# A 3x3 convolution on one core: four output pairs stored from ScalarE's DMA queue instead of one

## The chip, the core and the metric

The kernel runs on one core of one Trainium2 chip. The metric is device time in microseconds (us), as the median of several executions; the kernel before takes 127.07 us (three runs, 126.9 to 127.1). One execution was profiled, and all durations below come from it.

## The reference, cut to what matters

```python
x_pad = np.pad(x, ((0, 0), (0, 0), (1, 1), (1, 1)))       # x: 16 x 64 x 64 x 64, fp32
for b, co, ci, kh, kw:                                     # weight: 128 x 64 x 3 x 3, fp32
    output[b, co] += weight[co, ci, kh, kw] * x_pad[b, ci, kh:kh+64, kw:kw+64]
```

Sixteen images of 64 channels and 64x64 pixels are convolved with 128 filters of 3x3. 17.07 MB are read from HBM and 33.55 MB are written.

## The kernel before, in words

**Tiling.** Two images make a *pair*: their 2 x 64 channels fill the 128 partitions. There are eight pairs, and each is worked in two *halves*, so the main loop (line 206) has 16 steps (p, h). The vertical direction uses a small Winograd form, F(2,3): input rows are combined into sums (`ss`), differences (`dd`) and outer differences (`ee`) by GpSimd (lines 102 to 120; VectorE does it for the first half), and into an fp16 copy (`xh`, a cast on ScalarE, line 124). The filters are turned into seven fp16 matrices at the start.

**One half.** TensorE runs 54 matmuls into four PSUM tiles `pf1`, `pg1`, `pf2`, `pg2` of two banks each, all eight banks in total (lines 218 to 230). ScalarE makes three copies of PSUM tiles into `ut` (line 182), then the cast of the next half (line 226), then one copy straight into the output (line 234). VectorE makes the other three output rows by additions and subtractions (lines 231 to 233). All these instructions are kept in program order on their engine by `keep`. GpSimd works two halves ahead (line 208).

**Homes.** One SBUF tile `homes` has nine slots of 16 KB per partition. `X_HOME` says which slot holds pair p's input, and `O_HOME` which two adjoining slots hold its output. Slots are used again: the outputs of pairs 3, 4, 5 and 6 go to the slots that the outputs of pairs 0, 1, 2 and 3 left, those of pair 7 to a slot of pair 4's outputs and to the one where the input of pair 5 lay. So an output can be written only when the earlier store from its slot has landed.

**DMA order.** A DMA is issued by an engine's queue, in the order of that engine's program. SyncE (SP) issues the weights, the input of pair 0 in two parts, pairs 1 and 2, then pairs 3 and 4 as one transfer (line 72), all at the start. The inputs of pairs 5, 6 and 7 are issued from inside the loop, after the first halves of pairs 2, 3 and 4 (`NEXT_LOADS`, lines 53 and 237), since they take slots that other inputs must leave first. `store` (line 187) is called at the end of the second half of every pair. For the pairs in `BOTH` it is one transfer of 4 MB, for the others one transfer of 2 MB for each image. For pair 0 it is issued by ScalarE's queue, for all others by SP. In the second image of pair 5 the last seven rows are cut off and stored as 124 and 4 partitions (`FEW`). In the profile, SP's DMA queue is q1 and ScalarE's is q10.

Of the kernel before, what the change touches and what calls it, by code (L numbers as in the profile page):

```python
# [15 lines left out]
def kernel(  # L16
# [12 lines left out]
    nc = tc.nc  # L29
# [6 lines left out]
    keep = tc.keep_in_program_order  # L36
    x_rows = x.rearrange("b c h w -> (b c) h w")
# [10 lines left out]

    X_HOME = [0, 1, 2, 7, 8, 2, 7, 8]
    O_HOME = [5, 3, 0, 5, 3, 0, 5, 2]  # L50
    BOTH = (0, 3, 6)
    FEW = 5, 1, 7
    NEXT_LOADS = {(2, 0): 5, (3, 0): 6, (4, 0): 7}
    homes = slots.tile([128, 9, H, W], F32)
# [5 lines left out]
    def load(p, cuts=((0, H),)):  # L60
        for lo, hi in cuts:
            keep(
                nc.sync.dma_start(
                    xs[p][:, lo:hi, :], x_rows[128 * p : 128 * p + 128, lo:hi, :]
                )
            )
# [1 line left out]
    load(0, ((0, 34), (34, H)))  # L68
    load(1)
    load(2)  # L70
    rows = x_rows[128 * 3 : 128 * 5, :, :].rearrange("(g p) h w -> p g h w", g=2)
    keep(nc.sync.dma_start(homes[:, 7:9, :, :], rows))

    ident = const.tile([128, 128], F16)
    make_identity(nc, ident)
# [46 lines left out]
    def cast(p, h):  # L122
        t = cpool.tile([128, 17, W], F16, tag="xh", name="xh")
        keep(nc.scalar.copy(t, xs[p][:, C_ROW[h] : C_ROW[h] + 17, :]))  # L124
        return t

    def transforms(eng, p, h):
        return sums(eng, p, h), diffs(eng, p, h), outers(eng, p, h)
# [17 lines left out]
    def mms(tiles, terms, start, stop):  # L146
        n = 3 * len(terms)
        i = 0
        for wi, src, row in terms:
            for kw in (1, 0, 2):  # L150
                c_lo, c_hi = max(0, 1 - kw), min(W, W + 1 - kw)
                lo, hi = 0, RB
                at, step, rows = row
                while at + step * lo < 0:
                    lo += 1
                while at + step * (hi - 1) > rows - 1:
                    hi -= 1
                first, last = at + step * lo, at + step * (hi - 1)
                for b2 in range(2):
                    p0 = 64 * b2  # L160
                    keep(
                        nc.tensor.matmul(  # L162
                            tiles[:, b2, lo:hi, c_lo:c_hi],
                            Wt[p0 : p0 + 64, wi, kw, :],
                            src[
                                p0 : p0 + 64,
                                first : last + 1 : step,
                                c_lo + kw - 1 : c_hi + kw - 1,
                            ],
                            start=start and i == 0,  # L170
                            stop=stop and i == n - 1,
                            skip_group_check=not start,
                        )
                    )
                i += 1

    def acc():
        return psum.tile([128, 2, RB, W], F32, tag="acc", name="acc")

    def copied(tiles):  # L180
        ut = upool.tile([128, 2, RB, W], F32, tag="ut", name="ut")
        keep(nc.scalar.copy(ut, tiles))  # L182
        return ut
# [3 lines left out]
    def store(p, both):  # L187
        if p in BOTH:
            pair = out[2 * p : 2 * p + 2, :, :, :].rearrange("b c h w -> c b h w")

            eng = nc.scalar if p == 0 else nc.sync
            keep(eng.dma_start(pair, both))
            return
        for b2 in range(2):
            parts = [(0, CO, 0, H)]
            if (p, b2) == FEW[:2]:
                at = H - FEW[2]
                parts = [(0, CO, 0, at), (0, 124, at, H), (124, 4, at, H)]
            for c, n, lo, hi in parts:
                keep(  # L200
                    nc.sync.dma_start(
                        out[2 * p + b2, c : c + n, lo:hi, :], both[c : c + n, b2, lo:hi, :]
                    )
                )

    for n, (p, h) in enumerate(halves):
        if n + 2 < len(halves):
            tr[halves[n + 2]] = transforms(nc.gpsimd, *halves[n + 2])
        if h == 0:
            both = homes[:, O_HOME[p] : O_HOME[p] + 2, :, :]  # L210
            ov = both.rearrange("p b (j i) c -> p b j i c", i=2)
        ss, dd, ee = tr.pop((p, h))
        xc = xh.pop((p, h))
        jf, jg = RB * F_BLK[h], RB * G_BLK[h]
        sf, sg = jf - 16 * h, jg - 16 * h
        g_at = 2 * jg - C_ROW[h]

        pf1, pg1, pf2, pg2 = acc(), acc(), acc(), acc()
        mms(pf1, [(HP, ss, (sf, 1, 16))], True, True)
        ux = copied(pf1)  # L220
        mms(pg1, [(G1, ss, (sg, 1, 16))], True, True)
        ug = copied(pg1)
        mms(pf2, [(HM, dd, (0, 1, RB))], True, True)
        uy = copied(pf2)
        if n + 1 < len(halves):
            xh[halves[n + 1]] = cast(*halves[n + 1])
        mms(pg2, [(G01, xc, (g_at, 2, 17)), (G2, xc, (g_at + 2, 2, 17))], True, True)
        mms(pf1, [(G0, ee, (0, 2, 16))], False, True)
        mms(pg1, [(G21, xc, (g_at + 1, 2, 17)), (G0, xc, (g_at - 1, 2, 17))], False, True)
        mms(pf2, [(G2, ee, (1, 2, 16))], False, True)  # L230
        keep(nc.vector.tensor_add(ov[:, :, jg : jg + RB, 1, :], pg2, ug))  # L231
        keep(nc.vector.tensor_add(ov[:, :, jf : jf + RB, 0, :], pf1, uy))  # L232
        keep(nc.vector.tensor_sub(ov[:, :, jf : jf + RB, 1, :], ux, pf2))  # L233
        keep(nc.scalar.copy(ov[:, :, jg : jg + RB, 0, :], pg1))  # L234
        if h == 1:
            store(p, both)
        if (p, h) in NEXT_LOADS:
            load(NEXT_LOADS[p, h])

# [29 lines left out]
```

## Time and profile before

| what | value |
| --- | --- |
| median of three runs | 127.07 us |
| the profiled execution, its time | 126.95 us |
| its span, first to last instruction | 125.2 us |
| TensorE (PE) busy | 95.7 us |
| GpSimd (POOL) busy | 90.5 us |
| ScalarE (ACT) busy | 81.4 us |
| VectorE (DVE) busy | 63.9 us |
| DMA traffic | 50.77 MB, mean 406 GB/s |
| share of q1 (SP) and q10 (ACT) in the DMA engines' span | 88.6% and 7.9% |

The profiled execution's time is 1.75 us more than its span: what lies around the instructions. The page of the profile cuts the span into 40 slices of 3.13 us and gives a digit for the busy tenths of each engine, and under it the GB/s that the 16 DMA engines moved. The chain of waits follows the work back from the last instruction that an engine executed; transfers that are still running after that are not in it. The window view gives the same numbers for chosen stretches, the timeline lists instructions in order of time, and below it all the trace has a record of every packet that the DMA engines moved. In this kernel most packets are one row of 16 KB: one partition's 64x64 fp32 pixels.

### The profile page before, as it was taken

The page shows a single profiled execution, that of the slowest core. Times are in us where ns is not written, and L with a number is a line of the kernel's source. Part 1 is how long each engine was busy: PE and PEld are TensorE (multiplying, and loading weights), DVE is VectorE, ACT ScalarE, POOL GpSimd, SP SyncE. Part 2 cuts the span into 40 slices and gives each one's busy share as a digit, 9 for nine tenths or more (in the row PEclk, how much of TensorE's full clock was granted, in tenths as well). Part 3 has the DMA queues.
Part 4 walks back from the last instruction along what each step waited for, and adds up shares of the span by engine and source line. Part 5 has one row for each costly group of instructions (what it writes and reads, how often), then busy time and mean ns, then how long its engine had stood idle before and what let it go on. Part 6 is the DMA issues. An engine that isn't in the chain of part 4 may idle for free.

```text
span 125.2 us, 2157 instructions
## 1 busy us (share of the span) xinstructions
PE 95.7 (76%) x873; PEld 50.5 (40%) x873; DVE 63.9 (51%) x56; ACT 81.4 (65%) x86; POOL 90.5 (72%) x52
## 2 busy tenths in 40 slices
PE   0349999999999999999999999999999980000000
PEld 0224455455555555555555555555555530000000
DVE  0199657374939375674839393746647392000000
ACT  4457598599797978889897979788897940000000
POOL 2209999999999999999999999999999400000000
PEclk9999999999999999999999999999999997555555
DMA  4999999999999999999999999999999999999981
GB/s 125 375 454 424 429 429 429 435 335 419 424 429 435 435 419 429 403 437 440 437 411 382 440 424 419 429 440 424 435 419 431 426 414 436 429 440 435 419 372 58
DMA packets 3826, 50.77 MB, mean 406 GB/s; under 512 B 360, under 2 KB 488, under 8 KB 744
## 3 DMA queue, kind: packets, MB, share of 16 engines
q1 hardware_dynamic: 3544, 46.43, 88.6%
q10 hardware_dynamic: 272, 4.19, 7.9%
q8 instruction: 7, 0.11, 0.3%
q14 instruction: 3, 0.02, 0.0%
HBM read 17.07 MB, written 33.55 MB: 405 GB/s over the span
## 4 chain that ended last, share of the span: by engine, by line
PE 76%; DVE 3%; DMA 2%; POOL 1%; ACT 0%; issue 0%; DVEq 0%
PE acc L162 76%; DMA w_raw<-in_weight_dram 2%; DVE homes L233 1%; DVE ss L106 1%; POOL w L78 1%; DVE th L133 0%; DVE Wt L134 0%; PE wp L95 0%; ACT g0h L131 0%; DVEq L134 0%
## 5 line engine op out<-in xcount | busy, mean ns | idle before, releaser
L162 PEld LDWEIGHTS <-Wt 64*128 64x128 f16 x864 | 49.6, 96 | 47.0 <-issue 3.7
L182 ACT COPY ut<-acc 128x1024 f32<-128x1024 f32 x48 | 45.7, 1020 | 6.3 <-PE acc L162 6.3
L162 PE MATMUL acc<-xh,Wt 64*128 64x504 f16 (+3 forms) x384 | 46.3, 372 | 0.0
L106 POOL TENSOR_TENSOR ss<-homes 128x1024 f16<-128x1024 f32 x15 | 35.5, 2369 | 4.7 <-DMA homes<-in_x_dram 4.7
L231 DVE TENSOR_TENSOR homes<-acc,ut 128x1024 f32<-128x1024 f32 x16 | 19.6, 1225 | 32.2 <-PE acc L162 29.7
L119 POOL TENSOR_TENSOR ee<-homes 128x1024 f16<-128x1024 f32 x15 | 35.6, 2375 | 0.0
L162 PE MATMUL acc<-ss,Wt 64*128 64x504 f16 (+1 forms) x192 | 24.9, 392 | 2.3 <-DVE ss L106 2.3
L162 PE MATMUL acc<-ee,Wt 64*128 64x504 f16 (+1 forms) x192 | 26.5, 377 | 0.0
L234 ACT COPY homes<-acc 128x1024 f32<-128x1024 f32 x16 | 16.2, 1015 | 11.3 <-PE acc L162 10.7
L233 DVE TENSOR_TENSOR homes<-ut,acc 128x1024 f32<-128x1024 f32 x16 | 19.5, 1220 | 2.0 <-PE acc L162 1.4
L113 POOL TENSOR_TENSOR dd<-homes 128x512 f16<-128x512 f32 x15 | 20.2, 1347 | 0.0
L232 DVE TENSOR_TENSOR homes<-acc,ut 128x1024 f32<-128x1024 f32 x16 | 19.4, 1215 | 0.0
L124 ACT CAST xh<-homes 128x1088 f16<-128x1088 f32 x16 | 17.9, 1120 | 0.0
L162 PE MATMUL acc<-dd,Wt 64*128 64x504 f16 (+1 forms) x96 | 13.9, 392 | 0.0
L95 PE MATMUL wp<-ident,w 128*128 128x128 f16 x9 | 1.1, 309 | 4.6 <-POOL w L78 4.6
L133 DVE SCALAR_TENSOR_TENSOR th<-wp,g0h 128x384 f32<-128x384 f32 x1 | 0.6, 557 | 5.7 <-ACT g0h L131 5.7
L95 PEld LDWEIGHTS <-w 128*128 128x128 f16 x9 | 0.9, 158 | 4.6 <-POOL w L78 4.6
L119 DVE TENSOR_TENSOR ee<-homes 128x1024 f16<-128x1024 f32 x1 | 2.6, 2622 | 0.0
L78 POOL CAST w<-w_raw 128x576 f16<-128x576 f32 x1 | 0.7, 662 | 2.5 <-DMA w_raw<-in_weight_dram 2.5
L79 ACT CAST w<-w_raw 128x576 f16<-128x576 f32 x1 | 0.7, 672 | 1.8 <-DMA w_raw<-in_weight_dram 1.8
L79 ACT ACT_TABLE_LOAD x1 | 1.3, 1283 | 0.7 <-PEq L253 0.7
L106 DVE TENSOR_TENSOR ss<-homes 128x1024 f16<-128x1024 f32 x1 | 1.2, 1216 | 0.0
(15 smaller groups left out, 5.7 us busy)
## 6 DMA issues: line engine op xcount, KB each, us to landing
out_dram<-homes SPq DMA_DIRECT2D x9, 2048.0 KB, 17.5
homes<-in_x_dram SPq DMA_DIRECT2D x5, 2048.0 KB, 18.8
out_dram<-homes SPq DMA_DIRECT2D x2, 4096.0 KB, 22.2
homes<-in_x_dram SPq DMA_DIRECT2D x1, 4096.0 KB, 30.4
out_dram<-homes ACTq DMA_DIRECT2D x1, 4096.0 KB, 18.6
out_dram<-homes SPq DMA_DIRECT2D x1, 1824.0 KB, 23.6
homes<-in_x_dram SPq DMA_DIRECT2D x1, 1088.0 KB, 5.5
homes<-in_x_dram SPq DMA_DIRECT2D x1, 960.0 KB, 7.4
```

The costliest lines, as they stand in the source:

```text
L79: keep(nc.scalar.copy(w16[:, 1, :], w_raw))
L95: keep(nc.tensor.matmul(wps[kh][:, k * CO : k * CO + CO], w16[:, :, 3 * kh + k :: 9], ident))
L106: keep(eng.tensor_add(t, v[:, j : j + 16, 0, :], v[:, j : j + 16, 1, :]))
L113: keep(eng.tensor_sub(t, v[:, j : j + RB, 1, :], v[:, j : j + RB, 0, :]))
L119: keep(eng.tensor_sub(t, xs[p][:, r - 1 : r + 15, :], xs[p][:, r + 1 : r + 17, :]))
L124: keep(nc.scalar.copy(t, xs[p][:, C_ROW[h] : C_ROW[h] + 17, :]))
L162: nc.tensor.matmul(tiles[:, b2, lo:hi, c_lo:c_hi], Wt[p0 : p0 + 64, wi, kw, :], src[p0 : p0 + 64, first : last + 1 : step, c_lo + kw - 1 : ...
L182: keep(nc.scalar.copy(ut, tiles))
L231: keep(nc.vector.tensor_add(ov[:, :, jg : jg + RB, 1, :], pg2, ug))
L232: keep(nc.vector.tensor_add(ov[:, :, jf : jf + RB, 0, :], pf1, uy))
L233: keep(nc.vector.tensor_sub(ov[:, :, jf : jf + RB, 1, :], ux, pf2))
L234: keep(nc.scalar.copy(ov[:, :, jg : jg + RB, 0, :], pg1))
```

## The change

`BOTH` becomes (0, 2, 4, 6), and every store of these pairs is one 4 MB transfer issued by ScalarE's queue. It is no longer issued at the end of the pair but in the first half of the next pair, after the third PSUM copy and ahead of the cast. The pairs 1, 3, 5 and 7 stay on SP with one transfer for each image, pair 5 with its cut. The inputs of pairs 3 and 4 become two transfers. On SP, four stores and a merged load make way for that: between the input of pair 5 and that of pair 6 there is now no store, and between the stores of pairs 3 and 5 only the input of pair 7.

```diff
-    BOTH = (0, 3, 6)
+    BOTH = (0, 2, 4, 6)
...
-    rows = x_rows[128 * 3 : 128 * 5, :, :].rearrange("(g p) h w -> p g h w", g=2)
-    keep(nc.sync.dma_start(homes[:, 7:9, :, :], rows))
+    load(3)
+    load(4)
...
     def store(p, both):
         if p in BOTH:
             pair = out[2 * p : 2 * p + 2, :, :, :].rearrange("b c h w -> c b h w")
-
-            eng = nc.scalar if p == 0 else nc.sync
-            keep(eng.dma_start(pair, both))
+            keep(nc.scalar.dma_start(pair, both))
             return
...
         uy = copied(pf2)
+        if h == 0 and p - 1 in BOTH:
+
+            store(p - 1, before)
         if n + 1 < len(halves):
             xh[halves[n + 1]] = cast(*halves[n + 1])
...
-        if h == 1:
+        if h == 1 and p not in BOTH:
             store(p, both)
+        before = both
```

## The prediction

> **What bounds the kernel now.** I read the slices of the page first.
>
> ```profile
> PE   0349999999999999999999999999999980000000
> ...
> DMA  4999999999999999999999999999999999999981
> GB/s 125 375 454 424 429 429 429 435 335 419 424 429 435 435 419 429 403 437 440 437 411 382 440 424 419 429 440 424 435 419 431 426 414 436 429 440 435 419 372 58
> ```
>
> PE is full until slice 32 of 40 and then has nothing. The DMA engines are full from slice 1 to slice 37. The chain of waits is read next, with the one line that SP's timeline has after it:
>
> ```profile
> 8.09 94.56 PE acc L162 x864
> 102.64 0.02 issue
> 102.66 1.22 DVE homes L233
> ```
>
> ```profile
> 103.95 1.62 SPq L201 DMA_DIRECT2D out_dram<-homes  x2
> ```
>
> The chain says PE, but it ends at 103.9 us, and the span is 125.2. What comes after is the drain of stores. Is the drain late because the last store comes late, or because the queue is long? The windows tell:
>
> ```profile
> 38.00:48.00 10.00, 10.00 (x98) 5.38 (x96) 6.17 (x6) 8.20 (x10) 10.00 (x6) 1.00 1.01 431
> 104.00:120.00 16.00, 0.00 (x0) 0.00 (x0) 0.00 (x0) 0.00 (x0) 0.00 (x0) 0.52 1.01 433
> ```
>
> (The last column is GB/s.) The rate is 431 with compute running and 433 without, and at 433 the last pair's 4.19 MB need 9.7 us, yet they take about 19. So some 9 us of older stores stood ahead of them. In the trace's packet records no DMA engine has gaps of more than 0.6 us in total between 1.8 us and its end. **The bytes bound the kernel**: 50.77 MB at 430 GB/s are 118 us. Only three things can move the end: a hole in the DMA stream, slower packets, or a last DMA engine that ends at another time. The drain shows the third:
>
> ```profile
> 120.00:121.00 1.00, 0.00 (x0) 0.00 (x0) 0.00 (x0) 0.00 (x0) 0.00 (x0) 0.50 0.77 328
> 121.00:122.00 1.00, 0.00 (x0) 0.00 (x0) 0.00 (x0) 0.00 (x0) 0.00 (x0) 0.50 0.69 295
> 122.00:123.00 1.00, 0.00 (x0) 0.00 (x0) 0.00 (x0) 0.00 (x0) 0.00 (x0) 0.50 0.42 180
> 123.00:124.00 1.00, 0.00 (x0) 0.00 (x0) 0.00 (x0) 0.00 (x0) 0.00 (x0) 0.50 0.04 16
> ```
>
> The DMA shares sum to 1.92, so the engines end at 121.9 on average, while the last packet ends at 123.9: the span's end is that engine plus 1.3 us.
>
> **The change part by part.**
>
> *Bytes and transfers.* The bytes are the same, and so is the number of transfers, 24 (stores 15 to 14, input loads 8 to 9, weights 1). Cost 0.
>
> *Store 0, issued later.* Today:
>
> ```profile
> 21.37 1.01 ACT L234 COPY homes<-acc 128x1024 f32<-128x1024 f32 x1 [0.62 <-PE acc L162]
> 23.33 0.42 ACTq L192 DMA_DIRECT2D out_dram<-homes  x1
> 23.79 2.84 ACT L182 COPY ut<-acc 128x1024 f32<-128x1024 f32 x3 [1.41 <-PE acc L162]
> ```
>
> The issue waits for VectorE's last row, done at 23.24, and holds the three copies behind it from 22.66 (22.38 plus the usual 0.28) to 23.79. The change takes this 1.1 us from ScalarE; nobody gains, because PE has no gap there and is not the bound. After it the copies run 22.66 to 25.5 and the issue (0.42) starts between 24.5, when the third copy starts, and 25.5. Until the store's packets come, the engines have only the initial loads. Those would end at about 27.5: in the packet records an engine has six load packets of 0.61 us left at 23.9. Does the store come in time? The nearest start on idle engines is the weights: issued at 0.73, first packet 1.75, so 1.0 us; that gives 25.5 to 26.5, no hole. The store's own delay today is 3.75 us (23.33 to 27.08), which would give 28.3 to 29.3, a hole of 0.8 to 1.8 us. But this delay holds load packets that stood ahead on the same engines, and these are what ends at 27.5. I take the weights' row: **0, at most 1.8**. The Trainium skill ("DMA: Bandwidth & Descriptors", section "Latency and other measured facts") puts the first byte of a transfer issued by SP or ACT at about 0.6 us; by that the store would start by 26.1 and the sum would have no hole either, while the 3.75 of the trace speaks against reading 0.6 as the delay on loaded engines.
>
> *Change-over from loads to stores.* Where stores come in among loads, packets get slower:
>
> ```profile
> 25.30:27.00 1.70, 1.70 (x19) 0.86 (x17) 1.25 (x2) 1.70 (x3) 1.70 (x2) 1.00 1.10 337
> 27.00:28.50 1.50, 1.50 (x17) 0.86 (x15) 1.50 (x2) 1.50 (x3) 1.50 (x2) 1.00 0.92 350
> ```
>
> ```profile
> 65.00:69.00 4.00, 4.00 (x41) 2.12 (x39) 3.22 (x3) 3.10 (x4) 4.00 (x4) 1.00 0.98 389
> 78.00:83.50 5.50, 5.50 (x54) 2.89 (x52) 3.26 (x4) 4.60 (x6) 5.50 (x4) 1.00 1.01 432
> ```
>
> Against 430, the first two lose 1.7 x 93/430 + 1.5 x 80/430 = 0.65 us (store 0 on its own queue). Around 65 to 69 input 6 ends and store 3 begins in the same queue: 4 x 41/430 = 0.38. At 78 to 83.5 input 7 runs at full rate. After the change store 0 costs 0.65 again, or nothing if the loads are out. Store 2 now breaks in upon input 5 from the other queue: 0 (as input 7) to 0.65 (as store 0). Store 4 breaks in upon store 3, no load: 0. Inputs 6 and 7 alternate with stores; at 28.5 to 30, where both queues run, packets are back at 0.61 us, so 0 more. Bounds of the difference: -0.65 to +0.65. I take +0.3 for store 2, the middle, since neither row is nearer.
>
> *Input 7, later.* In the packet records both queues alternate packet by packet on one engine (store 27.2, load 27.8, store 28.5), so a store on q10 halves the pace of q1. Store 4 is issued with the third copy of (5,0), at 70.6 to 72, and begins by 71.6 to 75.7. At 74 q1 holds 9.4 us of store 3 and input 7 (its packets end at 83.4 now), and store 4 is 9.7 us: input 7's packets end near 93, at the latest 83.4 + 9.7 = 93.1.
>
> ```profile
> homes<-in_x_dram SPq DMA_DIRECT2D x1, 2048.0 KB, 21.9
> ```
>
> ```profile
> 86.46 2.36 POOL L106 TENSOR_TENSOR ss<-homes 128x1024 f16<-128x1024 f32 x1
> ```
>
> Issued at 63.07, it lands today at 85.0, and POOL takes it at 86.46: 1.5 us of slack. It will land at 91 to 94.7, so POOL stands still 4.5 to 8 us, and PE and ScalarE behind it (the cast of line 124 waits for it too, with the copies after it). POOL then needs 11.8 us for two halves, and 2.6 us of matmuls and 1.2 of VectorE follow: the last store is issued at 107 to 110 instead of 104. What hides it: stores 5 and 6 in the queues. Without it, an engine ends its last 9.7 us at the earliest at issue + 1.0 + 9.7, so 110 gives 120.7, before the 123.9 of the last engine. Cost 0; the cover is gone from 123.9 - 10.7 = 113 on.
>
> *Other waits.* Inputs 5 and 6 would land near 59 and 70, and POOL takes them at 62.97 and 74.72. Store 3 shares with store 4 and lands near 83; pair 6 writes its slots from 82.9: a second at most, inside the same cover. ScalarE's three new issues (0.42 each) fit in its 0.6 us of idle time per half.
>
> *The last engine.* It ends 2 us behind the mean by chance of slow packets (1.7 to 3.9 us of excess per engine) and by the cut of pair 5, which stays. Reshuffled: 0, at most 0.8 either way.
>
> **Sum**: 126.95 + 0 + 0.3 + 0 = 127.25; the median lies 0.12 above the profiled time, so 127.4.
>
> **The rivals.**
>
> *A, a hole behind the loads* (ScalarE's store reaches the engines 3.75 us after its issue even when they are idle): 127.07 + 0.3 + 1.3 = 128.7. For it: that delay. Against it: the load packets ahead.
>
> *B, smoother change-over, faster*: store 0 arrives just when the loads are out, at 27.5, and the 0.65 us of slow packets between 25.3 and 28.5 vanish; it decides if the first store packet comes right behind the last load packet. With store 2 at 0 and the last engine at half of its 0.8: 127.07 - 0.65 - 0.4 = 126.0. For it: the issue comes 1.2 to 2.2 us later, about as much as separates store 0's packets from the end of the loads. Against it: input 6's end, where the change-over inside one queue cost 0.38 as well.
>
> *C, input 7 uncovers the end*: if the last store is issued after 113, each us costs one. PE's granted clock falls from 1.00 to 0.50 at 104.8, 2 us after its last matmul, and in its first 4.5 us (8.0 to 12.5) PE got through 22 matmuls where later 72 took 7.4 us, half the pace. A stall of 5 us could so add 2 us of PE, 112 in all, and a bit more makes 127.07 + 0.3 + 1.5 = 128.9. The Trainium skill (same page, "Queues, rings and completion order") says that a DMA engine goes round its queues packet by packet; the alternation in the records agrees, and it is this rule that delays input 7.
>
> *D, the chain of waits is right and PE's end counts*: +4 us, 131. Against it: 9 us of queue ahead of the last store.
>
> **Chances.** Forecast 0.52 (own range 126.7 to 128.0), A 0.14, B 0.22, C 0.08, D 0.04. This kernel's measurement can tell 0.2%, 0.25 us. Of the forecast's part 0.10 are faster, 0.14 within, 0.28 slower; so faster 0.10 + 0.22 = 0.32, within 0.14, slower 0.28 + 0.14 + 0.08 + 0.04 = 0.54. The range reaches from B at 126.0 past A and C to 129.2, which is A with its full 1.8.
>
> **What would show it.** DMA slices at 9 throughout with q10 at four times its share; no dip to 0 near 28 us; POOL waiting 4 to 8 us for an input near 86; SP's last store at 107 to 110; the drain at 430 GB/s, ending near 124. A dip near 28 means A, full rate from 25 to 28 means B, empty slices near 111 mean C. I am wrong in kind if the rate itself changes where both queues run.

## The result, and the profile after

The changed kernel takes 128.8 us (median of four runs, 128.17 to 129.14) where the kernel before took 126.98 on the same chip (four runs, 126.73 to 127.10): a ratio of 1.0149, 95% interval 1.012 to 1.0178. Timed again on another chip it took 128.14 (127.12 to 131.21, eight runs) against 126.83: 1.0059 (1.0025 to 1.0092). The two intervals do not meet; the change costs 0.6 to 1.5%, and its executions lie further apart than those of the kernel before. All ratios here leave out executions more than 1.5% above the fastest of their kernel; three experiments (store 4 alone, store 6 back on SP, useless matmuls) had such an execution profiled, and it is used for what its trace shows, not for its time.

The profiled execution took 128.17 us, with a span of 126.4. The page's slices of it:

```profile
PE   0339999999999999999999999999921999940000
...
POOL 2209999999999999999999999995008998000000
PEclk9999999999999999999999999999996579999555
DMA  4999999999999999999999999999999989989992
GB/s 110 382 436 441 430 436 420 425 389 441 446 425 415 415 420 420 371 410 430 438 412 436 425 425 436 420 430 430 415 441 421 428 310 443 420 332 410 415 415 104
```

PE has a hole at slices 29 and 30 (92 to 98 us), POOL one just ahead of it, and PE's granted clock is down behind it. PE has nothing in the last four slices; before, it had nothing in the last seven. The DMA row has what it did not have before: two digits below 9 in the middle, slices 32 and 35, where the rate is 310 and 332 GB/s; slice 35 begins at 110.6 us, and empty slices near 111 were the prediction's sign for rival C. Slice 8 (25 to 28 us), where store 0 comes in, is at 389 instead of 335; slice 16 (51 to 54), where store 2 now breaks in upon input 5, is at 371. The queues' shares went where the change sends them: q10 from 7.9 to 31.4%.

The DMA issues of 63 to 64 us and the timeline behind them (start, duration, engine, instruction; in brackets the idle time before it and what ended it):

```profile
homes<-in_x_dram SPq DMA_DIRECT2D x1, 2048.0 KB, 31.5
```

```profile
95.19 2.35 POOL L106 TENSOR_TENSOR ss<-homes 128x1024 f16<-128x1024 f32 x1 [8.13 <-DMA homes<-in_x_dram]
97.58 2.74 PE L162 MATMUL acc<-ss,Wt 64*128 64x512 f16 x12 [5.06 <-POOL ss L106]
101.70 0.38 ACTq L190 DMA_DIRECT2D out_dram<-homes  x1
113.42 2.35 SPq L199 DMA_DIRECT2D out_dram<-homes  x2
```

Input 7, issued at 63.55, lands after 31.5 us, at 95.05 (before: 85.0). POOL stands still for 8.13 us, PE for 5.06 behind it. ScalarE stands too, and so it issues store 6 at 101.70, though the last row of pair 6 was done at 93.79 (VectorE, 92.57 + 1.22). The last store is issued at 113.42; I call this time T, and in the kernel before it was 103.95.

The windows (busy time and count of PE, PEld, DVE, ACT and POOL, then PE's clock, DMA share, GB/s):

```profile
50.00:54.00 4.00, 3.98 (x38) 1.67 (x36) 3.01 (x3) 3.09 (x4) 4.00 (x2) 1.00 0.99 358
95.00:101.00 6.00, 3.42 (x18) 1.36 (x19) 0.00 (x0) 3.66 (x4) 5.82 (x3) 0.58 1.01 429
101.00:104.00 3.00, 3.00 (x22) 1.34 (x20) 0.24 (x1) 2.38 (x3) 3.00 (x3) 0.69 0.82 297
...
111.00:113.00 2.00, 1.09 (x12) 0.29 (x6) 1.83 (x2) 1.01 (x1) 0.00 (x0) 1.00 0.89 369
113.00:115.00 2.00, 0.00 (x0) 0.00 (x0) 0.35 (x1) 0.00 (x0) 0.00 (x0) 1.00 0.74 303
```

At 101 to 104 the DMA engines run partly dry (share 0.82) because store 6 is not yet issued, at 111 to 115 because store 7 is not. PE did 18 matmuls in 3.42 us at a clock of 0.58; from 104 to 111, at 1.00, it did 67 in 6.92.

To set the losses against each other I take the *lag*: the time, less the bytes moved by then at 430 GB/s (from the packet records of q1 and q10). The records do not name the engine; the engines' ends and gaps are put together from them, packet behind packet, and the idle times are good to some 0.2 us.

| | before | after |
| --- | --- | --- |
| lag at 24, 30, 50, 54 us | 2.86, 3.58, 3.73, 3.84 | 2.97, 3.16, 3.41, 4.13 |
| lag at 70, 100 us | 4.31, 4.47 | 4.30, 4.54 |
| lag at 104, 112, 118 us | 4.57, 4.56, 4.54 | 5.41, 5.50, 6.53 |
| idle time of one DMA engine, 100 to 118 us | about 0 | about 1.4 |
| the engines' ends, mean and last (the prediction's mean, 121.9, came from shares) | 122.27, 123.86 | 124.30, 125.11 |

By 100 us nothing is lost on balance: what store 0 gained, store 2 took. Then 0.9 us go ahead of store 6 and 1.0 ahead of store 7, and the mean engine ends 2.0 us later. The last engine ends only 1.25 later, since the wait for the last store evens the engines out.

### The profile page after: what moved, and what is told of

Same layout as the page of the kernel before. It is cut to its first block, busy times and chain, and to the rows that moved or that the text cites. A ratio compares the mean times of both kernels' runs of the same rounds, so it can differ in the third digit from the quotient of the medians.

```text
span 126.4 us, 2158 instructions
## 1 busy us (share of the span) xinstructions
PE 99.6 (79%) x873; PEld 45.8 (36%) x873; DVE 64.1 (51%) x56; ACT 81.7 (65%) x86; POOL 90.6 (72%) x52
## 3 DMA queue, kind: packets, MB, share of 16 engines
q10 hardware_dynamic: 1088, 16.78, 31.4%
## 5 line engine op out<-in xcount | busy, mean ns | idle before, releaser
L162 PEld LDWEIGHTS <-Wt 64*128 64x128 f16 x864 | 44.8, 97 | 61.0 <-issue 12.5
L162 PE MATMUL acc<-xh,Wt 64*128 64x504 f16 (+3 forms) x384 | 47.2, 380 | 0.0
L162 PE MATMUL acc<-ss,Wt 64*128 64x504 f16 (+1 forms) x192 | 26.0, 407 | 7.5 <-POOL ss L106 5.1
L235 ACT COPY homes<-acc 128x1024 f32<-128x1024 f32 x16 | 16.2, 1012 | 14.0 <-PE acc L162 12.1
L162 PE MATMUL acc<-dd,Wt 64*128 64x504 f16 (+1 forms) x96 | 14.5, 409 | 0.1
## 6 DMA issues: line engine op xcount, KB each, us to landing
homes<-in_x_dram SPq DMA_DIRECT2D x7, 2048.0 KB, 24.6
```

Of the source, the lines that this page charges most:

```text
L162: nc.tensor.matmul(tiles[:, b2, lo:hi, c_lo:c_hi], Wt[p0 : p0 + 64, wi, kw, :], src[p0 : p0 + 64, first : last + 1 : step, c_lo + kw - 1 : ...
```

## The experiments

Two theories stood first. **C**, from the prediction: store 4 makes something in SP's queue late, and through that the last store (the expectations call it L). **M**, its rival: a second queue with large stores costs time as such. Two experiments undo the lateness in different ways, a third brings it about with store 4 alone.

*Input 7 on ScalarE's queue, ahead of store 4* (from the changed kernel):

```diff
-    NEXT_LOADS = {(2, 0): 5, (3, 0): 6, (4, 0): 7}
+    NEXT_LOADS = {(2, 0): 5, (3, 0): 6}
...
             store(p - 1, before)
+        if (p, h) == (4, 1):
+            keep(nc.scalar.dma_start(xs[7], x_rows[128 * 7 : 128 * 8, :, :]))
```

> The changed kernel, with input 7 issued by ScalarE's queue in the second half of pair 4, ahead of store 4 in the same queue, and no longer by SP. All four stores stay on ScalarE's queue. Theory L (input 7 is late because store 4 halves the pace of its queue, so PE stalls and the last store is issued at 113.4 instead of 104): input 7 lands near 82, POOL waits for no input after the first, the last store is issued near 104, no hole in the DMA stream after 100, time 126.5 to 127.3. Rival M (two queues that mix loads and stores cost packets their pace, or stores on ScalarE's queue cost as such): the mixing is still there, 128.3 to 129.0.

Measured: 126.72 us (126.49 to 127.49, ten runs) against 126.74, ratio 0.9998 (0.9977 to 1.002). Its list of waits, and its timeline:

```profile
DVE homes L234 <- DMA out_dram<-homes: 9.0, 2, 6.3
```

```profile
86.50 2.41 POOL L106 TENSOR_TENSOR ss<-homes 128x1024 f16<-128x1024 f32 x1
111.82 2.60 SPq L199 DMA_DIRECT2D out_dram<-homes  x2
```

POOL takes input 7 at 86.50 without a wait, and all of the loss is gone, although four stores still go by ScalarE's queue. T is not back at 104, however: VectorE waits 6.3 us for store 3 to leave the slots that pair 6 writes, since store 3 now shares the engines with store 4. So store 4 delays two things. At T = 111.82 a delay costs nothing.

*Store 4 back on SP* (from the changed kernel):

```diff
-    BOTH = (0, 2, 4, 6)
+    BOTH = (0, 2, 6)
```

> The changed kernel with pair 4 out of BOTH, so that store 4 goes by SP behind input 7, as two transfers at the end of the pair. Theory L: input 7 lands near 85 as before the change, the last store is issued near 104, time 126.6 to 127.4. Rival M: one of four stores less on ScalarE's queue, so about a quarter of the 1.8 us is gone: near 128.3.

Measured: 126.79 (126.56 to 127.31, ten runs) against 126.74, ratio 1.0003 (0.9984 to 1.0023). Its timeline:

```profile
86.39 2.38 POOL L106 TENSOR_TENSOR ss<-homes 128x1024 f16<-128x1024 f32 x1
104.04 1.58 SPq L199 DMA_DIRECT2D out_dram<-homes  x2
```

POOL takes input 7 at 86.39 without a wait, VectorE has no wait for a store either, and T is that of the kernel before. Stores 0, 2 and 6 on the second queue, with their later issue, cost nothing. M falls: with input 7 ahead of store 4, or with store 4 back on SP, nothing is paid, so the price hangs on store 4 running beside the input 7 that waits on SP. The Trainium skill ("DMA: Bandwidth & Descriptors", section "Issuing engines are not separate DMA queues") says that transfers started by several engines share the same DMA engines, and that this saves only time of issuing; both runs agree in that the second queue gained nothing (0.9998 and 1.0003).

*Store 4 alone on ScalarE's queue* (from the kernel before):

```diff
         uy = copied(pf2)
+        if (p, h) == (5, 0):
+            pair = out[8:10, :, :, :].rearrange("b c h w -> c b h w")
+            keep(nc.scalar.dma_start(pair, before))
...
-        if h == 1:
+        if h == 1 and p != 4:
             store(p, both)
+        before = both
```

> The kernel before, with the one difference that store 4 is issued by ScalarE's queue behind the third copy of (5,0), as one transfer. Theory L: input 7 lands near 95 and the last store is issued near 113, as in the changed kernel, so this one move brings all of the loss: 128.2 to 129.0. Store 6 is issued by SP at the end of its pair, so a hole near 102 is not expected. Rival M: one quarter of the loss, near 127.4.

Measured: 131.58 (128.57 to 133.02, four runs) against 126.74; the runs lie too far apart for an interval. The DMA row of its page (span 131.2) and its timeline:

```profile
DMA  5999999999999999899999999999999799615995
```

```profile
90.87 1.23 DVE L234 TENSOR_TENSOR homes<-acc,ut 128x1024 f32<-128x1024 f32 x1 [8.60 <-DMA out_dram<-homes]
100.98 2.34 POOL L106 TENSOR_TENSOR ss<-homes 128x1024 f16<-128x1024 f32 x1 [12.59 <-DMA homes<-in_x_dram]
119.05 0.83 SPq L201 DMA_DIRECT2D out_dram<-homes  x2
```

One moved store is enough: even the shortest of the four executions, 128.57, is 1.4% above the kernel before. In the profiled one, the longest, input 7, issued at 64.97, lands 6 us later than in the changed kernel: by the semaphore records the 16 engines finished their parts of it between 91.4 and 100.8, and the landing is that of the slowest. T is 119.05, and the DMA row falls to 1 ahead of the last store.

*Input 7 late by order alone* (from the kernel before; nothing but store 0 on ScalarE's queue):

```diff
-    NEXT_LOADS = {(2, 0): 5, (3, 0): 6, (4, 0): 7}
+    NEXT_LOADS = {(2, 0): 5, (3, 0): 6, (4, 1): 7}
```

> The kernel before with one difference: the load of input 7 is issued behind store 4 in SP's queue (after (4,1) instead of after (4,0)). No store moves to ScalarE's queue and no queues mix. Theory L: input 7 lands near 85.0 + 9.7 = 94.7 as in the changed kernel, GpSimd waits 8 us for it, the last store is issued at 111 to 113.5 and the time rises by 0.3 to 1.6 us over the kernel before, to 127.1 to 128.4. Rival M (mixing queues is the cost): no change, 126.6 to 127.0.

Measured: 127.03 (126.87 to 127.72, ten runs) against 126.66, ratio 1.0027 (1.0002 to 1.0051). Its timeline, and its windows:

```profile
95.12 2.34 POOL L106 TENSOR_TENSOR ss<-homes 128x1024 f16<-128x1024 f32 x1 [8.38 <-DMA homes<-in_x_dram]
113.30 0.83 SPq L201 DMA_DIRECT2D out_dram<-homes  x2
```

```profile
111.00:113.00 2.00, 0.98 (x10) 0.27 (x6) 1.83 (x2) 1.01 (x1) 0.00 (x0) 1.00 0.52 221
```

In a single queue, by being put behind store 4, input 7 is as late as in the changed kernel (95.12 and 95.19), T is the same (113.30 and 113.42), and the DMA engines run dry for about 1.9 us each ahead of store 7. The time lies between the two expectations and decides nothing by itself; the trace does. This is C without a second queue. It costs 0.27%, less than the change, so the lateness of input 7 is not the whole price. In the profiles the difference lies in the last engine: all 16 engines end within 0.16 us (124.00 to 124.16), where in the changed kernel the mean is 124.30 and the last 125.11.

*The two remedies together* (input 7 on ScalarE's queue, and `BOTH = (0, 2, 6)`):

> The changed kernel with both remedies: input 7 is issued by ScalarE's queue in the second half of pair 4, and store 4 goes by SP at the end of its pair. So neither input 7 nor store 3 shares its time with store 4. Theory L: neither GpSimd nor VectorE waits for a transfer after the first, the last store is issued at 104 to 106. The run with input 7 on ScalarE's queue had moved 0.5 us more of bytes than the kernel before at 100 us, and lost it in the stalls behind store 3; without them the time is 126.2 to 126.5 where the kernel before has 126.7. If the last of the 16 engines decides whatever the mean does: 126.5 to 127.0, no difference.

Measured: 127.14 (126.38 to 128.03, twelve runs) against 126.86, ratio 1.0021 (0.9987 to 1.0054). The expected gain did not come. T was 106.92, as VectorE still waited 4.0 us for store 3, beside which input 7 now ran. The lag at 100 us was 4.32, against 4.47 before; the last engine ended at 124.19, 2.1 us behind the mean. In this execution, what the stream gained, the last engine took back.

Two dry places were seen in the changed kernel, ahead of store 6 and ahead of store 7. Three experiments are meant to close them.

*Store 6 back on SP* (from the changed kernel):

```diff
-    BOTH = (0, 2, 4, 6)
+    BOTH = (0, 2, 4)
```

> The changed kernel with pair 6 out of BOTH: store 6 goes by SP at the end of its pair instead of behind the third copy of (7,0). The changed kernel has two holes in the DMA stream, 0.8 us at 101 to 104 (store 6 not yet issued) and 1.1 us at 112 to 116 (store 7 not yet issued). Theory L with the end set by the last store's issue alone: the first hole closes, the second grows by as much, the last store is still issued near 113, time 128.3 to 129.0. Rival H (each hole counts by itself): 0.8 us less, near 128.0.

Measured: 127.87 (126.86 to 130.16, ten runs) against 126.74, ratio 1.0066 (1.0037 to 1.0094). The hole at 101 to 104 is closed (lag 5.09 at 100, 5.22 at 104), but in its profiled execution VectorE waited 5.1 us for store 3 and POOL 10.8 for input 7, T was 116.26, and the engines then lay dry ahead of store 7 instead, about 3.8 us each.

*Pair 7 stored in two halves of 32 rows* (from the changed kernel), so that half of the last bytes is issued one half earlier:

```diff
-        if h == 1 and p not in BOTH:
+        if p == NP - 1:
+            lo = 32 * h
+            for b2 in range(2):
+                keep(nc.sync.dma_start(out[2 * p + b2, :, lo : lo + 32, :], both[:, b2, lo : lo + 32, :]))
+        elif h == 1 and p not in BOTH:
             store(p, both)
```

> The changed kernel, with the rows 0 to 31 of pair 7 stored at the end of its first half, and only the rows 32 to 63 at the end of its second. Input 7 is as late as in the changed kernel. Theory L (the end is the last store's issue plus what it moves, about 9.7 us of packets): what the last issue carries is halved to 4.9 us, and the earlier half fills the hole at 112 to 116; the hole at 101 to 104 (0.8 us) stays, so the time falls by about 1 us, to 127.4 to 128.0. Rival M (two queues that mix loads and stores cost the pace): no change, 128.4 to 129.0.

Measured: 127.99 (127.45 to 129.8, four runs) against 126.83, ratio 1.0088 (1.0053 to 1.0123). That is at the upper end of what was expected, and too near to the 128.14 of the changed kernel on the same chip to show a gain.

*Both together*:

> The changed kernel with both edits together: pair 6 is stored by SP in two transfers at the end of the pair (as in the run of store 6 on SP), and pair 7 in two halves of 32 rows, the first after (7,0) (as in the run of the early store 7). Input 7 and store 3 still come late. Theory U, the late input uncovers the DMA engines in two places, ahead of store 6 (its issue stands behind ScalarE's stalled copies, 0.8 us lost at 101 to 104 in the changed kernel's profile) and ahead of store 7 (1.0 us at 112 to 116), and closing one leaves the other to grow: with both closed the median is 126.7 to 127.3, ratio 0.999 to 1.004, and the moved bytes lag by no more than 0.4 us more at 118 than at 100, though POOL still waits 8 to 11 us for input 7. Rival R, something else about a second queue with four stores costs the time (slower packets, a more ragged end): the median stays at 127.8 to 128.3 as with either edit alone, ratio 1.006 or more.

Measured: 127.83 (127.52 to 128.71, six runs) against 126.59, ratio 1.0102 (1.006 to 1.0144). Its DMA row, and its list of waits:

```profile
DMA  4999999999999999999999999999999999999970
```

```profile
POOL ss L106 <- DMA homes<-in_x_dram: 14.7, 2, 9.7
```

The holes are gone, as the DMA row shows (idle time of an engine from 100 to 118 us: about 0), though POOL waits 9.7 us, and yet the time is not back. Theory U falls by its own measure, and the time is the one that rival R named; but R's reason, four stores on the second queue, does not fit input 7 on ScalarE's queue, where all four stores go that way at no price. In this execution the mean engine ended at 122.48, 0.2 later than before, and the last at 124.41, 0.55 later. Part of that may come from the experiment itself, whose last packets are rows of 8 KB instead of 16. So the dry engines are not the whole price, and what the rest is stays open.

*Useless matmuls ahead of (7,0)'s first ones* (from the changed kernel), to hold PE's clock up; they write a PSUM tile that the right matmuls then start afresh:

```diff
+        if (p, h) == (7, 0):
+            for _ in range(7):
+                mms(pf1, [(G1, xc_old, (0, 1, 17))], True, True)
         mms(pf1, [(HP, ss, (sf, 1, 16))], True, True)
```

> The changed kernel, with 42 matmuls of no use ahead of the first ones of (7,0), into the tile that these then overwrite: PE has work while GpSimd waits for input 7. Theory L with the clock in it (the stall of 5 us lets PE's clock fall to half, and (7,0) takes 8.3 us instead of 5.8): (7,0) takes about 6 us, the last store is issued near 111.5 instead of 113.4, and the time falls by 1 to 2 us, to 127.0 to 127.8. Rival (the clock has no part, GpSimd's two halves set the pace after input 7): 128.4 to 129.0.

Measured: 128.56 (126.81 to 131.02, ten runs) against 126.83, ratio 1.0084 (1.0048 to 1.0119). This is not the 127.0 to 127.8 that was expected, but it is inconclusive: in its profiled execution pair 6 waited for store 3, and the useless matmuls ran at 97.71 to 102.43, not inside the stall.

*The changed kernel again*:

> The changed kernel once more, so that the other kernels of this call have it beside them on the same chip: 128.2 to 129.1, with the last store issued near 113. Since input 7 has landed only when the slowest of the 16 DMA engines is through with it, single executions may be longer.

Measured: 128.14, as told above, just under what was expected. Its profiled execution (127.61 us, span 125.8) tells more about the clock than the experiment before it. Its timeline:

```profile
88.56 0.82 PE L162 MATMUL acc<-ss,Wt 64*128 64x512 f16 x6 [3.29 <-DVE homes L232]
95.89 2.36 POOL L106 TENSOR_TENSOR ss<-homes 128x1024 f16<-128x1024 f32 x1 [9.08 <-DMA homes<-in_x_dram]
98.30 1.47 PE L162 MATMUL acc<-ss,Wt 64*128 64x512 f16 x12 [1.73 <-POOL ss L106]
111.86 2.72 SPq L199 DMA_DIRECT2D out_dram<-homes  x2
```

POOL starts 0.7 us later than in the first profile, but PE had been delayed by store 3 and stood only 1.73 us before (7,0); the twelve matmuls take 1.47 us, not 2.74, and T comes 1.56 us earlier. Here the clock was lost as well, from 89.6 to 93.0, behind the 3.29 us for store 3, but it was back before (7,0). From POOL's start to T the first profile needs 18.2 us and this one 16.0: the clock lost in (7,0) was worth some 2.3 us of T.

Two experiments look at the change-over from loads to stores near 25 us.

*Store 0 behind the cast of (1,0)* (from the kernel before):

> The kernel before, with store 0 alone moved: it is issued by ScalarE's queue behind the cast in (1,0), at about 26, instead of 23.3, and as one transfer as before. By the cumulated bytes the changed kernel lost 0.4 us less than the kernel before at 25 to 30, where store 0 comes in among the last loads. If that is the change-over and nothing else gives it back: 126.2 to 126.5 where the kernel before has 126.74 on the same chip, 0.3 us less. If the last of the 16 DMA engines sets the end whatever the mean does: no difference, within 0.2%.

Measured: 126.71 (126.41 to 127.36, twelve runs) against 126.83, ratio 0.9992 (0.9974 to 1.001). It tells little, since the issue came at 23.63 and not near 26: ScalarE issued the DMA before the third copy (24.09) and the cast (24.99), which stand ahead of it in its program, had started.

*Store 0 on SP's queue too* (from the kernel before, so that all transfers share one queue):

> The kernel before with store 0 on SP's queue too, behind the initial loads: nothing is stored by ScalarE's queue and no two queues run side by side. Over the runs so far, the loss around 25 to 30 fell from about 0.9 us where store 0 was issued at 23.2 to 23.6 to 0.2 us where it was issued at 24.6 to 24.95. In one queue the change-over is that of input 6 and store 3, 0 to 0.4 us. Theory: the mean of the DMA engines gains 0.3 to 0.6 us and the time falls to 126.1 to 126.5, where the kernel before has 126.8. If the last of the 16 engines decides whatever the mean does: 126.5 to 126.9, no difference. Rival M (ScalarE's queue costs as such): the gain would be about a quarter of the change's loss, 0.3 us, and would show in the rate beyond 30 us.

Measured: 127.11 (126.45 to 128.35, twelve runs) against 126.66, ratio 1.0033 (1.0 to 1.0067); the gain that was expected did not come. Its window where store 0 comes in:

```profile
26.00:28.00 2.00, 2.00 (x22) 1.07 (x20) 2.00 (x2) 1.38 (x2) 2.00 (x1) 1.00 1.08 311
```

The slow packets are there in one queue as well: the lag grows by 0.81 us from 24 to 30, against 0.72 in the kernel before. The change-over is not a matter of the second queue.

## Why the prediction was right, and where it was wrong

The time, 128.8, lies inside the range of 126.0 to 129.2, and its side, slower, had the largest chance. But the likeliest case did not come. The time is that of **rival C** (128.9), which had 0.08, and the signs are C's. That the side and the range held is luck in good part: 0.28 of the 0.54 for slower were the forecast's own, which went by a loss at the change-over that came out at 0, and the range reached as far as 129.2 for rival A's sake.

*What bounds the kernel: right.* At 70 and at 100 us the lag of the two kernels is the same within 0.1, although the order of the transfers differs.

*Store 0, cost 0: right.* No hole came behind the loads. It was issued at 24.93, inside the 24.5 to 25.5 that were given, and the windows from 24 to 28.5 have 415 GB/s. Rival A fell.

*Change-over, +0.3: its size was wrong.* Store 0 lost 0.2 instead of 0.7 us, store 2 upon input 5 lost 0.7 (4 x 72/430, the row of 50 to 54). In the second profile of the same kernel it was the other way round (1.0 and 0.03). The sum, by the lag at 70 us, is 0 (4.30 and 4.24 against 4.31). Each of the two stores came out towards an end of its bounds of 0 to 0.65, or beyond it, and at opposite ends in the two profiles. Of rival B's gain of 0.65 the first profile had 0.5, and store 2 ate it; the second had none.

*Input 7, "cost 0": this is the step that failed.* Its mechanism was right: alternation packet by packet (from 76 to 92 us q1 and q10 moved some 200 and 225 GB/s), a stall of POOL, a late last store. Three of its terms were too small:

- The landing. "91 to 94.7" was worked out with the mean backlog of an engine, but a landing is the slowest engine's. The 16 engines finished their parts between 82.3 and 85.0 in the kernel before and between 89.9 and 95.0 here, so the spread grew from 2.7 to 5.1 us. It landed at 95.05, and at 95.2 to 100.8 in six other executions of kernels with store 4 on ScalarE's queue and input 7 behind it.
- The clock. It stood in rival C only. PE's clock was at half from 96.0 to 102.8; the first 36 matmuls of (7,0) took 6.47 us (97.58 to 104.05), those of (6,1) 3.81 (86.61 to 90.42), so 2.66 were lost. 95.19 + 11.8 + 2.6 + 1.2, the prediction's own sum, gives 110.8; the clock makes it the 113.42 that was measured, 3.4 us beyond the upper end of "107 to 110". The Trainium skill ("TensorE: Matmul & The Clock Gate", Part 1) has the clock fall to half after an idle window of about 3.4 us; the traces agree roughly: stalls of 5.06, 3.29 and (input 7 on ScalarE's queue) 3.13 us lost the clock, those of 1.86 (store 6 back on SP) and 1.73 did not.
- The cover. "Stores 5 and 6 in the queues" was to hide it, but store 6 was not in its queue. Its issue stands behind ScalarE's copies, ScalarE stood with PE, and it came at 101.70, 7.9 us after pair 6's last row. I had written that the stall reaches ScalarE, and had not followed it to the DMA that ScalarE issues behind its copies.

*"The cover is gone from 113 on": nearly right.* Here T is the last store's issue in the profiled executions of the kernels that change the late part of the stream and keep pair 7's store whole:

| kernel | T | span | span less T |
| --- | --- | --- | --- |
| before | 103.95 | 125.2 | 21.3 |
| store 4 back on SP | 104.04 | 125.0 | 21.0 |
| both remedies | 106.92 | 125.5 | 18.6 |
| input 7 on ScalarE's queue | 111.82 | 124.7 | 12.9 |
| after, second profile | 111.86 | 125.8 | 13.9 |
| input 7 late by order alone | 113.30 | 125.3 | 12.0 |
| after | 113.42 | 126.4 | 13.0 |
| useless matmuls | 115.51 | 128.0 | 12.5 |
| store 6 back on SP | 116.26 | 128.4 | 12.1 |
| store 4 alone | 119.05 | 131.2 | 12.2 |

Up to 111.8 T has no price by itself; from 113 on the span is T + 12 to 13, where 1.0 + 9.7 + 1.3 was predicted. But both profiles of the changed kernel lie 1.1 above their neighbours in T, and pair 7 in halves with store 6 on SP pays 1% with no engine dry. So T explains the long executions (128 and more), and of the short ones only a part.

*Other waits, "a second at most": wrong in size.* VectorE waited 2.2 us for store 3 in the first profile, 6.5 in the second, 8.6 with store 4 alone, 5.1 with store 6 back on SP. In the second profile it took the place of PE's wait for input 7 rather than adding to it (3.29 and 1.73 us against 5.06), and by itself it cost nothing (input 7 on ScalarE's queue).

*The last engine, 0 with 0.8 either way: right in size.* It ended 0.8 us behind the mean, and 1.6 in the kernel before.

*Rival D*: PE's end does set the time once it comes late enough, but it had some 9 us of slack, which the chain of waits does not show.

Open stays what keeps 1% where no engine runs dry, and why the executions of kernels with store 4 on ScalarE's queue and input 7 behind it differ so (127 to 133 us). More unequal shares of the engines would fit, but no run isolates them.

## What to carry to other kernels

A transfer put into a second queue took about half the pace from what waited in the first: before moving a store, look up which load and which slot stand behind it there, and move the load first (input 7 ahead of store 4 made the same change free). When a stall is called covered, check that the covering transfer is issued by then, and not by an engine that stands in the same stall; and add the clock that PE loses in it. Take a landing from the slowest DMA engine, not from the mean.

## What the runs showed of the hardware

- The loss at the change-over near 25 us went with the time of store 0's issue: 0.7 to 1.0 us of lag in seven profiles where it was issued at 22.6 to 23.7, 0.5 in three at 24.1 to 24.5, 0.2 to 0.4 in four at 24.6 to 24.95. This is seen, not tested.
- ScalarE issues a DMA before earlier instructions of its program have run: in the changed kernel store 0 at 24.93, and the third copy, which stands ahead of it in the program, started at 25.38. With store 0 behind the cast it ran ahead of the cast too (23.63 and 24.99).
- PE's clock, lost in the stall before 97.58, was back only at 102.8, some 5 us after PE took up work again. In nine profiles there are ten such stretches at half clock; they lasted 3.4, 6.8 or 10.2 us, and full clock was back 3.0 to 6.0 us after the first matmul.
